# Encoder layer in split fp32r on one core: all late low parts of weight tiles made on VectorE

## The chip, the cores and the metric

The kernel runs on one core of a Trainium2 chip. Its time is device microseconds of one execution. A time is the median of several executions; beside them one execution is taken with the hardware profiler, and that one has a time of its own.

## The reference

One layer of a hybrid encoder is applied to two groups with shared weights: a prompt of 512 tokens and a sample of 1024, width 1024. All values are fp32. Cut to what matters:

```python
h = rms_norm(x, g_pre) * (1 + scale) + shift
p = h @ w_in
a_val, a_glu, a_z, u, v, b_z, g_a, g_b = jnp.split(p, IN_SPLITS, axis=-1)
y_a = conv_branch(a_val, a_glu, a_z, ...)   # GLU, depthwise conv of 31, LayerNorm, silu, gate, projection
y_b = sgu_branch(u, v, b_z, ...)            # u * (w_s v + b) per chunk of 128, gate, projection
m = jax.nn.sigmoid(g_a) * y_a + jax.nn.sigmoid(g_b) * y_b
o = m @ w_out
return x + gate * rms_norm(o, g_post)
```

So there are eight 1024x1024 products for the combined projection, two for the branches' own projections and one for the output, each for 512 + 1024 tokens.

## The kernel before

**Products.** TensorE multiplies fp32r numbers, which hold less than an fp32. Each fp32 operand is therefore split into a high part (a cast to fp32r) and a low part (the operand less its high part, again as fp32r), and each product is made of three matmuls: high by high, high by low, low by high. A step for one block of 128 output channels is 24 matmuls of 128x128 by 128x512. A unit of weights is a tile of 128x1024 that SyncE loads into `raw`; ScalarE casts it into `hi` (L247), and `lo` = `raw` - `hi` is made in one of three ways. The rings of `raw`, `hi` and `lo` hold four tiles each.

**Three ways to the low part.** `unit_act` and `unit_dve` do it. With `by_dma` true, ScalarE writes the rounded negative of `raw` into `lo`, and a transfer issued by GpSimd adds `raw` to it (L254, L240). With `by_dma` equal to "gp", GpSimd subtracts (L250). With `by_dma` false, VectorE subtracts (L263, in `unit_dve`). Which way a unit goes is set by the number of its step: up to `CONV_END` = 72 by the transfer, from there on the even steps by GpSimd and the odd ones by VectorE. The weights of the sample's `pair`s (below) are made in their own way, and the change does not touch them.

**Order of the steps.** The prompt comes first, in 88 steps: its combined projection, and from step 72 the branches' own projection (`cproj`) and the output projection (`w_out`). The sample is cut into two halves of 512 tokens, `sa` and `sb`. `steps_v` makes v of `sa` and of `sb` (16 steps). Then 28 `pair`s make the other products of the sample: each multiplies two channel blocks for both halves with seven half-size products of 12 matmuls (X, Y, X, Z, X, Z, X, on the operands (0,0), (0,1), S2, S1, S3, S4, (1,1)). S1 to S4 are sums of quarters of the activation; the generator `prep2` makes S3, S1, S2 in four rounds, one for each slice of 128 rows: four sums (L938 to L941), a subtraction (L933) and two of L935 for the low parts. The fourth sum is stored, and `prep3` loads it again for S4 (L971). At the end come `post_B` of `sa` and `sb`, `post_A` of `sa`, `steps_o` of `sa`, `post_A` of `sb` and `steps_o` of `sb` (48 steps).

**Background work and the planner.** A planner in Python writes the program, in the order in which the engines then run it. It keeps clocks of its own (`clk["pe"]`, `clk["dve"]`, `clk["act"]`); `dv(cost, ...)` emits an instruction of VectorE and adds its cost. After each step it emits that step's own work on ScalarE and VectorE, and `fill` puts in pieces of background work (generators in the list `bg`) as long as VectorE's planned clock is behind a given time. The prompt's convolution, `prep2`, `prep3`, `late_ln` and other jobs of the sample are such work. If a step needs a job that isn't finished, `meet` (L1424) calls `force`, which runs that job to its end there: the first `pair` needs "S" with its third product (L1063), and the first step of `post_A` needs hA of its half (L1331). `late_ln` makes hA: L1261 multiplies a block by the gate, ScalarE casts it, L1253 makes its low part; eight blocks.

**Names that the prediction uses.** L549 to L561 are the LayerNorm of v at the end of `steps_v` (L545 on ScalarE reads its banks from PSUM). L1028 adds two products of a `pair`; L1077 to L1084 and L1100 make that `pair`'s weights. L404 to L407 are the convolution. L623 to L640 end the output projection of a half. L336 and L335 are small matmuls that spread a mean over the rows, L325 makes their low part. L572 mixes v along the tokens.

Of the kernel before, what the change touches and what calls it, by code (L numbers as in the profile page):

```python
# [17 lines left out]
F32 = mybir.dt.float32  # L18
# [3 lines left out]
ALU = mybir.AluOpType  # L22
# [21 lines left out]
CONV_END = 72  # L44
# [36 lines left out]
def layer_kernel(ctx: ExitStack, tc, x_p, x_s, xt_p, xt_a, xt_b, par, w_blk, w_v, cproj, sproj, w_out, w_ada, w_gate, wsT, bs,  # L81
# [13 lines left out]
    V, S, PE, SP, GP = nc.vector, nc.scalar, nc.tensor, nc.sync, nc.gpsimd  # L95

    def bank():
        return ps.tile([P, T], F32, tag="b", name="b")

    def wk(n=T, dt=F32):  # L100
        return wkp.tile([P, T], dt, tag="wk", name="wk")[:, :n]

    def slot():
        return s16.tile([P, NK, T], F32, tag="s", name="S")
# [10 lines left out]
    def tok(t):  # L115

        return t.rearrange("p (i h) d -> p i (h d)", i=4)
# [10 lines left out]
    def dv(cost, fn):  # L128
        fn()
        clk["dve"] += cost  # L130
# [72 lines left out]
    steps = []  # L203
# [9 lines left out]
    def part_tile(n):  # L213
        return ring.tile([P, D], F32R, tag=n, name=n)

    live = {"raw": 0}
# [17 lines left out]
    def have(u):  # L234
        while u.raw is None:
            unit_load(loadq.pop(0)[1])

    def lo_by_dma(lo, src):

        GP.dma_start(lo.bitcast(F32), src, accum_op=ALU.add)  # L240

    def unit_act(u):
        if u.hi is None:
            have(u)
            u.hi = part_tile("hi")
            u.lo = part_tile("lo")
            S.copy(u.hi, u.raw)  # L247
            clk["act"] += 0.96
            if u.by_dma == "gp":
                GP.tensor_tensor(out=u.lo, in0=u.raw, in1=u.hi.bitcast(F32), op=ALU.subtract)  # L250
                u.raw = True
                live["raw"] -= 1
            elif u.by_dma:
                S.activation(u.lo, u.raw, AF.Copy, scale=-1.0)  # L254
                clk["act"] += 0.96
                lo_by_dma(u.lo, u.raw)
                u.raw = True
                live["raw"] -= 1
# [187 lines left out]
    def mm_cols(dst, u, act):  # L446
        wh3 = u.hi.rearrange("p (k c) -> p k c", k=NK)
        wl3 = u.lo.rearrange("p (k c) -> p k c", k=NK)
        for k in range(NK):
            if k == NK // 2:  # L450
                poll(clk["pe"] - PLAIN / 2)
            hi, lo = act.hi(k), act.lo(k)
            PE.matmul(dst, lhsT=wh3[:, k, :], rhs=hi, start=(k == 0), stop=False)  # L453
            PE.matmul(dst, lhsT=wh3[:, k, :], rhs=lo, start=False, stop=False)  # L454
            PE.matmul(dst, lhsT=wl3[:, k, :], rhs=hi, start=False, stop=(k == NK - 1))  # L455

    def mm_quarter(dst, wh, wl, act, q):
        for i in range(2):
            k = 2 * q + i
            hi, lo = act.hi(k), act.lo(k)  # L460
            PE.matmul(dst, lhsT=wh[:, i, :], rhs=hi, start=(k == 0), stop=False)
            PE.matmul(dst, lhsT=wh[:, i, :], rhs=lo, start=False, stop=False)
            PE.matmul(dst, lhsT=wl[:, i, :], rhs=hi, start=False, stop=(k == NK - 1))
# [28 lines left out]
    def add_step(st, *units):  # L492

        steps.append(st)
        st.units = units
        return st

    def col_step(t, src, act, a1=None, d1=None, d2=None, a2=None, pre=None, box=None, need=None, by_dma=True):
        u = Unit(src, len(steps), by_dma and (len(steps) < CONV_END or (len(steps) % 2 == 0 and "gp")))

        def mm():
            b = bank()
            mm_cols(b, u, act())
            box[0] = b

        st = add_step(Step(mm, a1, d1, a2, d2, pre, need=need), u)

        def quarter(b, wh, wl, q):
            box[0] = b
            mm_quarter(b, wh, wl, act(), q)  # L510
        st.quarter = quarter
        return st
# [15 lines left out]
    def steps_v(t, need=None):  # L528

        for h in range(2):  # L530
            banks = []
            for kc in range(4):
                u = Unit(w_v[h, kc], len(steps), True if len(steps) < CONV_END else len(steps) % 2 == 0 and "gp")

                def mm(u=u, kc=kc, banks=banks):
                    if kc == 0:
                        banks[:] = [bank() for _ in range(4)]
                    mm_rows(banks, u, t.operand(), kc)

                def a1(h=h, banks=banks):  # L540
                    if h == 0:
                        t.v = t.v_home()
                        t.bn = smp.tile([P, 4, 12], F32, tag="bn", name="bn", bufs=1)
                    for i in range(4):
                        S.activation(t.v[:, i, h * T:(h + 1) * T], banks[i], AF.Gelu_apprx_tanh)  # L545

                def d1(h=h):
                    for i in range(4):
                        dv(0.65, lambda: V.bn_stats(out=t.bn[:, i, h * 6:h * 6 + 6], in_=t.v[:, i, h * T:(h + 1) * T]))  # L549

                def d2(h=h):
                    if h == 0:
                        return
                    mv = smp.tile([P, 4, 2], F32, tag="mv", name="mv")
                    for i in range(4):
                        dv(0.15, lambda: V.bn_aggr(out=mv[:, i, :], in_=t.bn[:, i, :].rearrange("p (c s) -> p c s", s=6)))
                    var = smp.tile([P, 4], F32, tag="ss", name="var")
                    dv(0.1, lambda: V.tensor_copy(var, mv[:, :, 1]))
                    r = rstd_small(var, 4, LN_EPS)
                    for i in range(4):  # L560
                        dv(0.65, lambda: V.tensor_scalar(t.v[:, i, :], t.v[:, i, :], mv[:, i, 0:1], r[:, i:i + 1],  # L561
                                                         op0=ALU.subtract, op1=ALU.mult))
                    if t.after_v:
                        t.after_v()
                last = kc == 3
                add_step(Step(mm, a1 if last else None, d1 if last else None, None, d2 if last else None,
                              act=2.2 if last else 0.0, need=need if h == 0 and kc == 0 else None), u)
# [20 lines left out]
    def steps_o(t, final, on_end=None):  # L588

        for h in range(2):  # L590
            banks = []
            for kc in range(4):
                u = Unit(w_out[h, kc], len(steps), True if len(steps) < CONV_END else len(steps) % 2 == 0 and "gp")

                def mm(u=u, h=h, kc=kc, banks=banks):
                    if kc == 0:
                        banks[:] = [bank() for _ in range(4)]
                    if final and h == 1 and kc >= 1:
                        t.wl.append(u)
                        if kc == 3:  # L600
                            for i in range(4):
                                for c in (1, 2, 3):
                                    mm_rows(banks, t.wl[c - 1], t.m, c, (i,))
                        return
                    mm_rows(banks, u, t.m, kc)

                def a1(h=h, kc=kc, banks=banks):
                    if kc == 3:
                        if h == 0:
                            t.o = tok(slot())  # L610
                            t.q = smp.tile([P, 2, 4], F32, tag="q", name="q")
                        junk = wk()
                        for i in range(4):
                            S.activation(junk, banks[i], AF.Square, scale=1.0 / 32, accum_out=t.q[:, h, i:i + 1])

                def d1(h=h, kc=kc, banks=banks):
                    if kc == 3:
                        if h == 1 and final:
                            out_last(t, banks)
                            return  # L620
                        c = slice(h * T, h * T + T)
                        for i in range(4):
                            dv(0.6, lambda: V.tensor_mul(t.o[:, i, c], banks[i], G[t.g][:, c]))  # L623
                        if h == 1:
                            bg.insert(0, out_gen(t))
                st = add_step(Step(mm, a1, d1, act=2.3 if kc == 3 else 0.0), u)
                if h == 0 and kc == 0:
                    def start():
                        out_load(t)
                        t.o_begun = True  # L630
                    st.extra = start
# [856 lines left out]
    raw = {}  # L1488
# [134 lines left out]
    for q in range(4):  # L1623
        for j in range(NH):
            u = q * NH + j
# [215 lines left out]
```

## Time and profile before

| | us |
|---|---|
| median of three executions | 1452.87 (1452.58 to 1463.46) |
| the profiled execution | 1456.93 |
| its span | 1455.2 |
| TensorE busy in it | 1430.6 |
| VectorE busy | 1195.0 |
| ScalarE busy | 703.4 |
| GpSimd busy | 252.2 |

The span runs from the first instruction to the last; the remaining 1.7 us of the execution lie around it. L12 is line 12 of the kernel; `b` is a bank of PSUM, `wk` a tile of 128x512, `A` an operand for TensorE with its high and low part, `c` a tile of convolution or v. In a row of single instructions stand start, duration, engine, line, operation, and in brackets the idle time before it and what ended that. In a row of waits stand the total, the number of waits and the longest. In a row of stretches stand the start and end, the length, the busy time of TensorE, its weight loads, VectorE, ScalarE and GpSimd (the number of instructions in brackets), the granted clock of TensorE, the share of the DMA engines and GB/s.

### The profile page before, as it was taken

The numbers are of one execution on the slowest core, as the hardware profiler recorded it, in microseconds if no ns is written. First come the engines' busy times: TensorE is split into PE (matmuls) and PEld (weight loads), VectorE is DVE, ScalarE is ACT, GpSimd is POOL, SyncE is SP. The second block draws the span as 40 slices with busy tenths as digits, with TensorE's granted clock in tenths as the row PEclk, the third lists the DMA queues.
The fourth block names the chain that finished last, engine by engine and source line by source line (L and its number), as shares of the span: only waits on it lengthen the run. The fifth ranks groups of instructions, "written<-read, shape, count | busy, mean of one in ns | idle before, by whom it ended". The sixth has DMA issues, their size and how long they took to land.

```text
span 1455.2 us, 17663 instructions
## 1 busy us (share of the span) xinstructions
PE 1430.6 (98%) x6332; PEld 1169.5 (80%) x6332; DVE 1195.0 (82%) x1600; ACT 703.4 (48%) x1020; POOL 252.2 (17%) x216
## 2 busy tenths in 40 slices
PE   8999999999999999999999999999999999999997
PEld 4688888888878888888888888788888887888886
DVE  6769999975348876967999997899999969789855
ACT  4533644554475343454455555455556544444432
POOL 0001111111112221111111111111111122222120
PEclk9999999999999999999999999999999999999999
DMA  9277986898995556666667877898887797455451
GB/s 340 84 217 194 233 212 166 200 255 183 255 251 177 215 183 246 231 164 198 168 140 184 211 187 185 245 254 227 229 234 192 192 304 272 161 219 184 153 206 58
DMA packets 113703, 298.60 MB, mean 205 GB/s; under 512 B 12624, under 2 KB 16336, under 8 KB 112848
## 3 DMA queue, kind: packets, MB, share of 16 engines
q1 hardware_dynamic: 88992, 229.85, 46.0%
q0 software_dynamic: 24624, 67.64, 25.6%
q8 instruction: 49, 0.80, 0.2%
q14 instruction: 38, 0.31, 0.1%
HBM read 182.10 MB, written 47.71 MB: 158 GB/s over the span
## 4 chain that ended last, share of the span: by engine, by line
PE 74%; DVE 10%; DMA 9%; issue 3%; ACT 2%; SPq 1%; DVEq 0%; ACTq 0%; POOLq 0%
PE b L455 10%; PE b L453 10%; PE b L454 10%; PE b L487 9%; PE b L489 9%; PE b L488 9%; PE b L476 4%; PE b L477 4%; PE b L478 4%; DMA wk<-d 3%; DMA raw<-in_w_blk_dram 2%; DVE c L407 2%; PE b L572 1%; DMA raw<-in_w_v_dram 1%; DMA c<-d 1%
## 5 line engine op out<-in xcount | busy, mean ns | idle before, releaser
L487 PE MATMUL b<-A,hi 128*128 128x512 f32 x784 | 306.8, 391 | 3.9 <-ACT wk L1024 3.7
L488 PE MATMUL b<-A,hi 128*128 128x512 f32 x784 | 306.0, 390 | 0.0
L489 PE MATMUL b<-A,lo 128*128 128x512 f32 x784 | 306.0, 390 | 0.0
L453 PE MATMUL b<-A,hi 128*128 128x512 f32 x776 | 303.2, 391 | 0.0
L455 PE MATMUL b<-A,lo 128*128 128x512 f32 x776 | 302.1, 389 | 0.1
L454 PE MATMUL b<-A,hi 128*128 128x512 f32 x776 | 302.1, 389 | 0.0
L407 DVE SCALAR_TENSOR_TENSOR c<-c,prm 128x1024 f32<-128x1024 f32 x240 | 297.7, 1281 | 0.6
L247 ACT CAST hi<-raw 128x1024 fp32r<-128x1024 f32 x145 | 152.2, 1050 | 244.8 <-DMA raw<-in_w_v_dram 67.1
L487 PEld LDWEIGHTS b<-A,hi 128*128 128x128 f32 x784 | 147.8, 189 | 35.7 <-ACT wk L1024 5.1
L488 PEld LDWEIGHTS b<-A,hi 128*128 128x128 f32 x784 | 147.9, 189 | 30.9 <-DVE A L971 0.2
L489 PEld LDWEIGHTS b<-A,lo 128*128 128x128 f32 x784 | 147.7, 188 | 30.6
L455 PEld LDWEIGHTS b<-A,lo 128*128 128x128 f32 x776 | 145.7, 188 | 31.0 <-DMA lo<-raw 0.6
L454 PEld LDWEIGHTS b<-A,hi 128*128 128x128 f32 x776 | 145.7, 188 | 30.3 <-issue 0.2
L453 PEld LDWEIGHTS b<-A,hi 128*128 128x128 f32 x776 | 145.7, 188 | 30.2 <-issue 0.2
L407 DVE SCALAR_TENSOR_TENSOR S<-c,prm,S 128x512 f32<-128x512 f32 x240 | 162.5, 752 | 0.4
L250 POOL TENSOR_TENSOR lo<-raw,hi 128x1024 fp32r<-128x1024 f32 x40 | 103.8, 2596 | 329.9 <-ACT hi L247 322.3
L240 POOL DMA_DIRECT2D lo<-T x84 | 72.6, 865 | 456.6 <-ACT lo L1089 366.9
L476 PE MATMUL b<-hi,A 128*128 128x512 f32 x384 | 150.6, 392 | 0.0
L477 PE MATMUL b<-lo,A 128*128 128x512 f32 x384 | 149.8, 390 | 0.0
L478 PE MATMUL b<-hi,A 128*128 128x512 f32 x384 | 149.7, 390 | 0.0
L240 POOL DMA_DIRECT2D lo<-raw x87 | 75.4, 866 | 383.7 <-ACT lo L254 359.4
L1024 ACT COPY wk<-b 128x512 f32<-128x512 f32 x112 | 65.7, 586 | 125.3 <-PE b L489 117.3
(207 smaller groups left out, 1766.0 us busy)
## 6 DMA issues: line engine op xcount, KB each, us to landing
raw<-in_w_blk_dram SPq DMA_DIRECT2D x105, 512.0 KB, 5.3
d<-wk SPq DMA_DIRECT2D x142, 256.0 KB, 3.2
lo<-raw POOLq DMA_DIRECT2D x59, 512.0 KB, 6.1
wk<-d SPq DMA_DIRECT2D x116, 256.0 KB, 5.2
lo<-T POOLq DMA_DIRECT2D x28, 512.0 KB, 4.6
lo<-T POOLq DMA_DIRECT2D x56, 256.0 KB, 4.5
raw<-in_w_v_dram SPq DMA_DIRECT2D x24, 512.0 KB, 5.8
raw<-in_sproj_dram SPq DMA_DIRECT2D x24, 512.0 KB, 5.0
```

Of the source, the lines that this page charges most:

```text
L240: GP.dma_start(lo.bitcast(F32), src, accum_op=ALU.add)
L247: S.copy(u.hi, u.raw)
L407: lambda: V.scalar_tensor_tensor(acc, in0=win, scalar=wt, in1=acc, op0=ALU.mult, op1=ALU.add))
L453: PE.matmul(dst, lhsT=wh3[:, k, :], rhs=hi, start=(k == 0), stop=False)
L454: PE.matmul(dst, lhsT=wh3[:, k, :], rhs=lo, start=False, stop=False)
L455: PE.matmul(dst, lhsT=wl3[:, k, :], rhs=hi, start=False, stop=(k == NK - 1))
L476: PE.matmul(banks[i], lhsT=hi, rhs=wh3[:, kk, :], start=(k == 0), stop=False)
L477: PE.matmul(banks[i], lhsT=hi, rhs=wl3[:, kk, :], start=False, stop=False)
L478: PE.matmul(banks[i], lhsT=lo, rhs=wh3[:, kk, :], start=False, stop=(k == NK - 1))
L487: PE.matmul(dst, lhsT=wh3[:, k, :], rhs=hi, start=st, stop=False, skip_group_check=True)
L488: PE.matmul(dst, lhsT=wh3[:, k, :], rhs=lo, start=False, stop=False, skip_group_check=True)
L489: PE.matmul(dst, lhsT=wl3[:, k, :], rhs=hi, start=False, stop=sp, skip_group_check=True)
```

## The change

The branch in which GpSimd subtracts is taken out of `unit_act`. The units that took it (40, which are half of those from step 72 on: 8 of the prompt's last 16 steps, 8 of the two `steps_v`, 24 of the last 48 steps) are now made by VectorE in `unit_dve`, and the planner adds 1.14 to VectorE's clock for each, where it added nothing to any clock for GpSimd's.

```diff
@@ -246,11 +246,7 @@
             u.lo = part_tile("lo")
             S.copy(u.hi, u.raw)
             clk["act"] += 0.96
-            if u.by_dma == "gp":
-                GP.tensor_tensor(out=u.lo, in0=u.raw, in1=u.hi.bitcast(F32), op=ALU.subtract)
-                u.raw = True
-                live["raw"] -= 1
-            elif u.by_dma:
+            if u.by_dma:
                 S.activation(u.lo, u.raw, AF.Copy, scale=-1.0)
                 clk["act"] += 0.96
                 lo_by_dma(u.lo, u.raw)
@@ -496,7 +492,7 @@
         return st
 
     def col_step(t, src, act, a1=None, d1=None, d2=None, a2=None, pre=None, box=None, need=None, by_dma=True):
-        u = Unit(src, len(steps), by_dma and (len(steps) < CONV_END or (len(steps) % 2 == 0 and "gp")))
+        u = Unit(src, len(steps), by_dma and len(steps) < CONV_END)
 
         def mm():
             b = bank()
@@ -530,7 +526,7 @@
         for h in range(2):
             banks = []
             for kc in range(4):
-                u = Unit(w_v[h, kc], len(steps), True if len(steps) < CONV_END else len(steps) % 2 == 0 and "gp")
+                u = Unit(w_v[h, kc], len(steps), len(steps) < CONV_END)
 
                 def mm(u=u, kc=kc, banks=banks):
                     if kc == 0:
@@ -590,7 +586,7 @@
         for h in range(2):
             banks = []
             for kc in range(4):
-                u = Unit(w_out[h, kc], len(steps), True if len(steps) < CONV_END else len(steps) % 2 == 0 and "gp")
+                u = Unit(w_out[h, kc], len(steps), len(steps) < CONV_END)
 
                 def mm(u=u, h=h, kc=kc, banks=banks):
                     if kc == 0:
```

Since the clocks change, the planner puts other work at other places. Lines behind the first hunk have numbers four lower in the changed kernel. Two places on VectorE follow. The first is the passage from `steps_v` of `sb` to the first `pair`. Before, the last round of `prep2` stood between the two halves of v of `sb`, whose first L549 is the top row here:

```order
L549 BN_STATS bn<-c_4796 128x6 x4
L263 TENSOR_TENSOR lo<-raw,hi 128x1024
L938 TENSOR_TENSOR wk<-wk 128x512
L939 TENSOR_TENSOR wk<-wk 128x512
L940 TENSOR_TENSOR wk<-wk 128x512
L941 TENSOR_TENSOR wk<-wk 128x512
L1077 TENSOR_TENSOR T_4850<-raw 128x512
L1078 TENSOR_TENSOR T_4850<-raw,T_4850 128x512
L1100 TENSOR_TENSOR lo<-raw,hi 128x1024
L933 TENSOR_TENSOR A<-wk,A 128x512
L935 SCALAR_TENSOR_TENSOR A<-wk,s_t,A 128x512
L1083 TENSOR_TENSOR T_4885<-raw 128x512
```

and behind the end of v (L561) came the work of the first `pair` and S4 (L971):

```order
L561 TENSOR_SCALAR c_4796<-c_4796,mv,r 128x1024 x4
L1028 TENSOR_TENSOR wk<-b,wk 128x512
L1077 TENSOR_TENSOR T_5033<-raw 128x512
L1078 TENSOR_TENSOR T_5033<-raw,T_5033 128x512
L1100 TENSOR_TENSOR lo<-raw,hi 128x1024
L1083 TENSOR_TENSOR T_5071<-raw 128x512
L1084 TENSOR_TENSOR T_5071<-raw,T_5033 128x512
L971 TENSOR_TENSOR A<-wk,A 128x512
L1032 TENSOR_TENSOR wk<-wk 128x512
```

After the change, behind the end of v (now L557):

```order
L557 TENSOR_SCALAR c_4768<-c_4768,mv,r 128x1024 x4
L1024 TENSOR_TENSOR wk<-b,wk 128x512
L1073 TENSOR_TENSOR T_5007<-raw 128x512
L1074 TENSOR_TENSOR T_5007<-raw,T_5007 128x512
L1096 TENSOR_TENSOR lo<-raw,hi 128x1024
L934 TENSOR_TENSOR wk<-wk 128x512
L935 TENSOR_TENSOR wk<-wk 128x512
L936 TENSOR_TENSOR wk<-wk 128x512
L937 TENSOR_TENSOR wk<-wk 128x512
L929 TENSOR_TENSOR A<-wk,A 128x512
L931 SCALAR_TENSOR_TENSOR A<-wk,s_t,A 128x512 x2
```

The round of four sums (L934 to L937 now), the subtraction and the two of L931 have moved from ahead of v's end to behind the first weights of the first `pair`.

The second place is the end of `steps_o` of `sa`, ahead of `post_A` of `sb`. Before, the last pieces of hA (L1261, L1253) stood ahead of the second L623:

```order
L263 TENSOR_TENSOR lo<-raw,hi 128x1024
L1261 TENSOR_TENSOR wk<-wk,c_10114 128x512
L1253 TENSOR_TENSOR A<-wk,A 128x512
L1261 TENSOR_TENSOR wk<-wk,c_10114 128x512
L1253 TENSOR_TENSOR A<-wk,A 128x512
L1261 TENSOR_TENSOR wk<-wk,c_10114 128x512
L1253 TENSOR_TENSOR A<-wk,A 128x512 x2
L623 TENSOR_TENSOR S<-b,G_9838 128x512 x4
L640 SCALAR_TENSOR_TENSOR ss<-q 128x4
```

After the change the second L623 is L619, and ahead of it stand only these pieces of hA:

```order
L1257 TENSOR_TENSOR wk<-wk,c_10141 128x512 x2
L259 TENSOR_TENSOR lo<-raw,hi 128x1024
L1249 TENSOR_TENSOR A<-wk,A 128x512
L1257 TENSOR_TENSOR wk<-wk,c_10141 128x512
L1249 TENSOR_TENSOR A<-wk,A 128x512
L619 TENSOR_TENSOR S<-b,G_9837 128x512 x4
L636 SCALAR_TENSOR_TENSOR ss<-q 128x4
```

and behind it, after the ten small operations that end in L165:

```order
L165 SCALAR_TENSOR_TENSOR r<-u,r 128x4
L259 TENSOR_TENSOR lo<-raw,hi 128x1024
L1257 TENSOR_TENSOR wk<-wk,c_10141 128x512
L1249 TENSOR_TENSOR A<-wk,A 128x512
L1257 TENSOR_TENSOR wk<-wk,c_10141 128x512
L1249 TENSOR_TENSOR A<-wk,A 128x512
L1257 TENSOR_TENSOR wk<-wk,c_10141 128x512
L1249 TENSOR_TENSOR A<-wk,A 128x512
L1257 TENSOR_TENSOR wk<-wk,c_10141 128x512
L1249 TENSOR_TENSOR A<-wk,A 128x512
L1257 TENSOR_TENSOR wk<-wk,c_10141 128x512
L1249 TENSOR_TENSOR A<-wk,A 128x512 x2
L643 SCALAR_TENSOR_TENSOR S<-S,r 128x1024 x4
```

Five of the eight L1257 (L1261 before) and six of the eight L1249 (L1253 before) have moved behind it.

## The prediction

> **What bounds the kernel now.** I read the page first (span, busy times), then TensorE's waits, then the table by stretches.
>
> ```profile
> span 1455.2 us, 17663 instructions
> PE 1430.6 (98%) x6332; PEld 1169.5 (80%) x6332; DVE 1195.0 (82%) x1600; ACT 703.4 (48%) x1020; POOL 252.2 (17%) x216
> ```
>
> ```profile
> PE b L487 <- ACT wk L1024: 3.7, 2, 3.3
> ...
> PE b L336 <- DVE wk L325: 2.3, 3, 1.4
> PE b L572 <- DVE c L561: 1.8, 4, 1.1
> ```
>
> ```profile
> 500.00:600.00 100.00, 98.24 (x432) 80.96 (x431) 76.19 (x104) 41.31 (x63) 22.14 (x9) 0.98 0.62 215
> 600.00:700.00 100.00, 100.00 (x499) 84.83 (x498) 73.09 (x114) 46.70 (x72) 15.40 (x16) 1.00 0.72 202
> 900.00:1000.00 100.00, 96.61 (x414) 79.13 (x413) 88.05 (x101) 53.26 (x84) 17.27 (x20) 0.97 0.88 237
> 1160.00:1400.00 240.00, 238.04 (x1047) 196.16 (x1047) 203.18 (x250) 108.66 (x158) 57.44 (x25) 1.00 0.65 225
> ```
>
> TensorE (PE) is busy for 1430.6 of 1455.2 us; the second number of a stretch is its busy time. The program ends when TensorE ends, so a change off TensorE matters only through its gaps. All it could still remove in these four stretches is 1.8 + 0.0 + 3.4 + 2.0 = 7.2 us (100 or 240 less its busy time). No wait for a subtracted low part stands among the large ones: what the change touches is not late now.
>
> **The change part by part.** The execution shown took 1456.93 us (span and 1.7 around it), 4.1 above the median of 1452.87. I work with differences and put them on both.
>
> *Forty subtractions move.*
>
> ```profile
> L250 POOL TENSOR_TENSOR lo<-raw,hi 128x1024 fp32r<-128x1024 f32 x40 | 103.8, 2596 | 329.9 <-ACT hi L247 322.3 <-PE b L478 7.6
> L263 DVE TENSOR_TENSOR lo<-raw,hi 128x1024 fp32r<-128x1024 f32 x46 | 56.2, 1221 | 30.7 <-ACT hi L247 30.7
> ```
>
> GpSimd loses 103.8 us; nothing waits for that. VectorE gains 40 x 1.22 = 48.8 us, and perhaps 40 x 30.7/46 = 27 us of waiting at these rows for the cast of the high part. Against this stands what GpSimd's subtractions cost VectorE:
>
> ```profile
> 579.89 2.88 DVE L938 TENSOR_TENSOR wk<-wk 128x512 f32<-128x512 f32 x1
> 596.05 0.69 DVE L938 TENSOR_TENSOR wk<-wk 128x512 f32<-128x512 f32 x1
> L522 DVE TENSOR_TENSOR A<-wk,A 128x512 fp32r<-128x512 f32 x16 | 15.8, 990 | 10.4 <-ACT A L519 10.4
> L1261 DVE TENSOR_TENSOR wk<-wk,c 128x512 f32<-128x512 f32 x16 | 15.1, 952 | 0.0
> ```
>
> The same instruction takes 0.69 us, or 2.88 with a GpSimd subtraction beside it. The last two rows are groups of the stretch 1160 to 1456, where 24 of the 40 run: with 0.69 us for one, their excess is 16 x (0.30 + 0.26) = 9 us. That is a floor for 24 of them, so 15 for 40; the ceiling is one full delay each, 40 x 2.19 = 88. I take the middle, 52, since other lines are stretched too. VectorE then gets 3 us less busy, but waits up to 27 more: between 39 us freed (88 - 49) and 61 lost (49 + 27 - 15), spread over some 450 us in which it idles about a fifth (76.19, 73.09 of 100, 203.18 of 240). By itself I cost this at nothing: idle VectorE hides it, and where that cover is gone it shows as the two gaps below. The Trainium skill, "SBUF — State Buffer", section "SBUF: two separate sides", says that a VectorE instruction with two SBUF inputs and a GpSimd instruction that reads SBUF exclude each other for a whole instruction; 2.88 against 0.69 agrees. By that rule alone the sum would be a small gain; it is the first rival.
>
> *The planner's order moves, and this has the price.* Each moved subtraction charges 1.14 us to the planner's VectorE clock, which was charged nothing for GpSimd's. So `fill` puts less background work between the steps, and a job not finished is pulled in by `meet` only where its step stands.
>
> *Place A, the first product that needs S2.* `meet` pulls the whole last round of the operand S (four sums, one subtraction, two of L935) in behind the second half of the sample's v, as the rows of the order in the section on the change show. Durations, all from before:
>
> ```profile
> 615.89 0.68 DVE L938 TENSOR_TENSOR wk<-wk 128x512 f32<-128x512 f32 x1
> 618.66 0.68 DVE L1077 TENSOR_TENSOR T<-raw 128x512 f32<-128x512 f32 x1
> 621.13 0.68 DVE L933 TENSOR_TENSOR A<-wk,A 128x512 fp32r<-128x512 f32 x1
> 621.73 0.74 DVE L935 SCALAR_TENSOR_TENSOR A<-wk,s_t,A 128x512 fp32r<-128x512 f32 x1
> 633.23 0.39 PE L487 MATMUL b<-A,hi 128*128 128x512 f32 x1
> 633.43 0.60 ACT L545 ACTIVATE c<-b 128x512 f32<-128x512 f32 x1 [0.76 <-PE b L478]
> 634.06 0.69 DVE L549 BATCH_NORM_STATS2 bn<-c 128x6 f32<-128x512 f32 x1 [0.42 <-ACT c L545]
> 637.52 2.98 DVE L561 TENSOR_SCALAR c<-c,mv,r 128x1024 f32<-128x1024 f32 x4
> 640.41 0.69 DVE L1028 TENSOR_TENSOR wk<-b,wk 128x512 f32<-128x512 f32 x1
> 643.48 0.68 DVE L1083 TENSOR_TENSOR T<-raw 128x512 f32<-128x512 f32 x1
> ```
>
> Let E = 633.23 be where v's last matmul gives way to the pair. Everything from L549 on hangs on E (last bank, L545, L549, the small ones, L561). Where before runs L1083, at E + 10.25, the round now begins: four sums 2.77 (615.89 to 618.66), L933 0.60 (621.13 to 621.73), two of L935 at 0.7 each: S2 is there at E + 15.0. TensorE has 34 matmuls before it needs that last slice: the first two products of 12, and three slices of three and one more. At 0.227 us each (below, 1359.08 to 1361.35 for ten) this is E + 7.7. The gap is 7.3 us. Before, it had S2 at 621.73 and soon after, ahead of E, and TensorE is busy 100.00 of this 100 us.
>
> *What hangs behind A.* S4 is loaded back from what the fourth sum of this round stores:
>
> ```profile
> d<-wk SPq DMA_DIRECT2D x142, 256.0 KB, 3.2
> ...
> wk<-d SPq DMA_DIRECT2D x116, 256.0 KB, 5.2
> ```
>
> From E + 13.0 this is 13.0 + 3.2 + 5.2 = E + 21.4, with a cast and a subtraction (0.6 each) E + 22.6; TensorE wants it after 26 more matmuls, at E + 15.0 + 5.9 = E + 20.9 at the earliest, its last slice 9 matmuls later at E + 22.9, and later with a slow clock: no further gap counted.
>
> *What a gap costs beyond itself.*
>
> ```profile
> 920.81 0.39 PE L489 MATMUL b<-A,lo 128*128 128x512 f32 x1
> 924.46 0.80 PE L487 MATMUL b<-A,hi 128*128 128x512 f32 x1 [3.26 <-ACT wk L1024]
> 925.05 0.63 PE L488 MATMUL b<-A,hi 128*128 128x512 f32 x1
> 929.74 0.53 PE L487 MATMUL b<-A,hi 128*128 128x512 f32 x1
> ```
>
> After a gap of 3.65 us, TensorE took 5.28 us for the 12 matmuls up to 929.74, which take 2.72 otherwise, in the stretch with granted clock 0.97: 2.6 us more. So A costs 7.3 + 2.6 = 9.9; without the slow stretch 7.3. The Trainium skill, "TensorE: Matmul & The Clock Gate", section "What's actually happening", states half rate after an idle window of about 3.4 us, until some 3.4 us of work; by that a gap costs about 1.7 us more (an estimate from that page) instead of 2.6. The sum would be 0.9 lower; the row decides.
>
> *Place B, the first step of post_A for the sample's second half.* Its operand hA is made by L1261 and L1253, eight of each. Before, the last ran at 1356.32. Now eleven of them stand behind the second half of L623, its small operations and one subtraction.
>
> ```profile
> 1354.65 0.69 DVE L1261 TENSOR_TENSOR wk<-wk,c 128x512 f32<-128x512 f32 x1
> 1355.25 0.69 DVE L1253 TENSOR_TENSOR A<-wk,A 128x512 fp32r<-128x512 f32 x1
> 1356.32 2.47 DVE L1253 TENSOR_TENSOR A<-wk,A 128x512 fp32r<-128x512 f32 x1 [0.39 <-ACT A L1262]
> 1359.08 0.39 PE L476 MATMUL b<-hi,A 128*128 128x512 f32 x1
> 1359.76 0.39 PE L453 MATMUL b<-A,hi 128*128 128x512 f32 x1
> 1361.35 0.39 PE L454 MATMUL b<-A,hi 128*128 128x512 f32 x1
> 1360.74 0.69 DVE L623 TENSOR_TENSOR S<-b,G 128x512 f32<-128x512 f32 x1 [0.16 <-ACT wk L614]
> 1363.44 1.23 DVE L263 TENSOR_TENSOR lo<-raw,hi 128x1024 fp32r<-128x1024 f32 x1
> ```
>
> With E2 = 1359.76 as the end of the step before, L263 ends at 1364.67 = E2 + 4.9 (L623 needs the last bank, so this can't be earlier). Then 11 x 0.60 = 6.6 (1354.65 to 1355.25): the eighth slice is ready at E2 + 11.5. TensorE reaches the third slice at E2 + 6 x 0.227 = 1.4, finds it at E2 + 6.1 and then goes at VectorE's pace; three matmuls after the last slice give E2 + 12.2 to 12.8 instead of 24 x 0.227 = 5.45. B costs 7.1 on average of these; 4.7 if only the first gap counts, 7.4 with slow matmuls to the end.
>
> *What is gained.* The waits at L561 (1.8) and at L336 (2.3) stand where VectorE is behind GpSimd's subtractions. At best both go (with the slow matmuls that follow the first, up to 5.4 together), at worst none: I take 2.5. The wait at L1024 (3.3, with its slow matmuls 3.65 + 2.6 = 6.2) hangs on transfers and stays: 0, between -6.2 and +6.2.
>
> Sum: 9.9 + 7.1 - 2.5 = 14.5 us: 1452.87 + 14.5 = 1467.4, and 1471.4 against the execution shown. Ends without the wait at L1024: 7.3 + 4.7 - 5.4 = 6.6 and 9.9 + 7.4 - 0 = 17.3, so 1459.5 to 1470.2.
>
> **The rivals.**
> First, the other side: VectorE is ahead. The same rows of GpSimd (2.88 against 0.69) are what it is held by; if the relief nears 88 us, and the background work that `fill` puts later is done in time all the same, A and B don't open and the gaps at L561 and L336 go: 1452.87 - 5.4 = 1447.5, up to about 1454. For it: VectorE idles a fifth of these stretches. Against: at both places the late work is chained to E and E2, whatever VectorE did earlier; it decides only if the round stands ahead of L549, which the new order doesn't show. 0.10.
> Second, the gaps open but are shorter: part of the chain overlaps, the clock stays up. 7.3 + 4.7 - 2.5 = 9.5, so 1459 to 1463. 0.17.
> Third, one more gap of the same make, where another job is pulled in late (the pairs after A, the sample's convolution). Priced by the row at 924.46, 3.65 + 2.6 = 6.2: 1473.6. For it: VectorE is 88.05 busy of 100 there, and forty charges of 1.14 shift everything behind. 0.15.
> That the change doesn't do what it says: the branch is gone and VectorE has forty more rows; GpSimd still issues its transfers. 0.01.
>
> **How the numbers follow.** The forecast, both gaps at 1463 to 1471, gets 0.57. The range reaches from the shorter gaps to the near half of the third rival, 1458 to 1474: 0.57 + 0.16 + 0.08 = 0.81. One per cent, about what a measurement of this kernel can tell from no change, is 14.5 us: 1438.3 and 1467.4. My sum lies on the upper line, so the forecast splits into halves. Slower: 0.28 + the third rival 0.14 + 0.02 of others = 0.44. Faster by 14.5 us would need more than the gaps that are left: 0.03. Within: 0.53.
>
> **What would show it.** In the changed profile, whose line numbers are four lower from the edit on: no POOL TENSOR_TENSOR, 46 + 40 rows of VectorE's subtraction at about 1.22; no L938 or L1261 at 2 to 3 us (now L934, L1257); a wait of TensorE for VectorE's L931 (L935 before) of some 7 us in the first pair, with matmuls 0.43 apart behind it; another of 4 to 5 at L449 for L1249; and a granted clock below 1 in these two stretches. A wrong prediction would show TensorE's busy time up with no such waits, waits at the subtractions themselves (L259), or S2 ready in time, with the round ahead of L549.

## The result, and the profile after

| | us |
|---|---|
| before, median of six executions taken with it | 1455.04 (1452.58 to 1463.46) |
| after, median of six executions | 1467.9 (1465.37 to 1469.57) |
| ratio | 1.0083, 95% interval 1.0064 to 1.0101 |
| after, the profiled execution | 1467.77 (before: 1456.93) |

The change costs 12.9 us by the medians; the ratio says 0.83%. The page of the changed kernel (span, busy times) and its table of TensorE's waits (total, times, longest):

```profile
span 1466.1 us, 17639 instructions
...
PE 1432.4 (98%) x6332; PEld 1169.7 (80%) x6332; DVE 1178.2 (80%) x1640; ACT 702.0 (48%) x1020; POOL 148.9 (10%) x176
```

```profile
PE b L450 <- DVE A L1249: 5.8, 1, 5.8
PE b L483 <- ACT A L923: 5.5, 1, 5.5
...
PE b L483 <- ACT wk L1020: 1.9, 4, 0.9
...
PE b L484 <- DVE A L931: 1.1, 1, 1.1
```

VectorE has 40 instructions more and is busy 16.8 us less (1195.0 to 1178.2). No wait of TensorE for a weight's subtraction (L259) is in this table. The new waits are the two that the prediction placed: the operand S2 in the first pair (L923 makes its high part, L931 its low part), and hA at `post_A` (L1249). The stretches show where VectorE became freer and TensorE idler all the same:

```profile
500.00:600.00 100.00, 100.00 (x455) 83.27 (x454) 72.33 (x113) 41.58 (x63) 0.00 (x0) 1.00 0.64 221
600.00:700.00 100.00, 93.35 (x455) 78.70 (x454) 69.88 (x110) 45.49 (x70) 11.45 (x13) 0.97 0.66 188
900.00:1000.00 100.00, 98.91 (x435) 81.22 (x435) 91.62 (x105) 54.91 (x87) 18.40 (x21) 1.00 0.89 247
1160.00:1400.00 240.00, 232.75 (x1013) 190.74 (x1012) 187.44 (x264) 107.50 (x157) 2.58 (x3) 0.99 0.64 216
```

From 600 to 700 us VectorE's busy time falls from 73.09 to 69.88 and TensorE's from 100.00 to 93.35; from 1160 to 1400 from 203.18 to 187.44 and from 238.04 to 232.75. If TensorE waited because VectorE had too much to do, VectorE would be busier here than before, not less busy.

Both traces hold 6332 matmuls, so the start of the n-th can be compared. The difference, after less before, changes only in these stretches (times are those of before):

| stretch | gain or loss of the stretch, us | what is there |
|---|---|---|
| 0 to 456 us | +2.6 | a small matmul at 425 us (L331, L335 before) waits 0.45 us longer; behind it the granted clock is 0.50 for 3.4 us |
| 456 to 609 us | -4.4 | the gap of 1.5 us at 591 us is gone |
| 609 to 668 us | +9.2 | place A |
| 668 to 933 us | -6.6 | the gap of 3.65 us at 921 us is gone (and 0.4 us at 913 us) |
| 933 to 1201 us | +2.9 | small gaps, the largest at 965 us (1.29) and 1052 us (0.95) |
| 1201 to 1226 us | -1.1 | the gap of 1.8 us at 1203 us is gone |
| 1226 us to the end | +8.3 | place B |

The sum is 10.8 us, as the two profiled executions differ (1467.77 - 1456.93). Each trace is one execution, and that of before took 1.9 us more than its median, so the terms add up to 10.8 and not to 12.9.

Place A in single instructions, first TensorE, then VectorE:

```profile
631.38 0.39 PE L483 MATMUL b<-A,hi 128*128 128x512 f32 x1
...
638.63 0.39 PE L485 MATMUL b<-A,lo 128*128 128x512 f32 x1
644.56 0.80 PE L483 MATMUL b<-A,hi 128*128 128x512 f32 x1 [5.54 <-ACT A L923]
646.46 0.79 PE L484 MATMUL b<-A,hi 128*128 128x512 f32 x1 [1.10 <-DVE A L931]
```

```profile
635.66 2.98 DVE L557 TENSOR_SCALAR c<-c,mv,r 128x1024 f32<-128x1024 f32 x4
...
641.62 0.68 DVE L934 TENSOR_TENSOR wk<-wk 128x512 f32<-128x512 f32 x1
...
645.00 1.41 DVE L931 SCALAR_TENSOR_TENSOR A<-wk,s_t,A 128x512 fp32r<-128x512 f32 x2
```

E is 631.38 here. The round of S begins at E + 10.24 (forecast 10.25) and S2 is whole at 646.41, E + 15.03 (forecast 15.0). TensorE runs 33 matmuls, stops at 638.63 and is idle 5.93 + 1.90 less two spacings of 0.23, 7.4 us (forecast 7.3). The rest of the 9.2 us is slow matmuls.

Place B, TensorE, then VectorE and ScalarE:

```profile
1362.26 0.39 PE L449 MATMUL b<-A,hi 128*128 128x512 f32 x1
...
1363.62 0.39 PE L449 MATMUL b<-A,hi 128*128 128x512 f32 x1
1369.85 0.80 PE L450 MATMUL b<-A,hi 128*128 128x512 f32 x1 [5.84 <-DVE A L1249]
```

```profile
1362.51 2.85 DVE L619 TENSOR_TENSOR S<-b,G 128x512 f32<-128x512 f32 x4 [1.37 <-ACT wk L610]
...
1367.37 1.22 DVE L259 TENSOR_TENSOR lo<-raw,hi 128x1024 fp32r<-128x1024 f32 x1
...
1369.11 0.68 DVE L1249 TENSOR_TENSOR A<-wk,A 128x512 fp32r<-128x512 f32 x1
...
1373.93 1.46 DVE L1249 TENSOR_TENSOR A<-wk,A 128x512 fp32r<-128x512 f32 x2
```

```profile
1360.57 0.62 ACT L1258 CAST A<-wk 128x512 fp32r<-128x512 f32 x1
1361.10 0.81 ACT L1244 ACTIVATE c<-c,prm 128x512 f32<-128x512 f32 x1
1361.82 0.58 ACT L610 ACTIVATE wk<-b 128x512 f32<-128x512 f32 x1
```

E2 is 1362.26. The third slice is there at E2 + 7.5 and not at E2 + 6.1, the last at E2 + 13.1 and not at 11.5. The difference stands ahead of L619: VectorE waits 1.37 us for L610 (ScalarE's square of a bank), which runs late behind casts and activations of the same moved job (L1258, L1244). Before, the first three of its four instructions (L623) began ahead of E2 = 1359.76:

```profile
1358.71 1.87 DVE L623 TENSOR_TENSOR S<-b,G 128x512 f32<-128x512 f32 x3
```

Of the 8.3 us at this place 6.0 are the gap (6.23 less one spacing of 0.23). Behind it 1.9 are matmuls 0.43 apart, and 0.4 are waits of the weight loads for the last slices.

### The profile page after: what moved, and what is told of

Read it like the earlier page. It is cut to its first block, busy times and chain, and to the rows that moved or that the text cites. A ratio compares the mean times of both kernels' runs of the same rounds, so it can differ in the third digit from the quotient of the medians.

```text
span 1466.1 us, 17639 instructions
## 1 busy us (share of the span) xinstructions
PE 1432.4 (98%) x6332; PEld 1169.7 (80%) x6332; DVE 1178.2 (80%) x1640; ACT 702.0 (48%) x1020; POOL 148.9 (10%) x176
## 4 chain that ended last, share of the span: by engine, by line
PE 57%; DVE 6%; DMA 3%; issue 1%; ACT 1%; SPq 1%; DVEq 0%; ACTq 0%
PE b L483 10%; PE b L484 10%; PE b L485 10%; PE b L473 5%; PE b L474 5%; PE b L472 5%; PE b L450 4%; PE b L451 4%; PE b L449 4%; DMA wk<-d 2%; PE b L568 1%; DVE c L403 1%; DVE wk L1175 1%; DVE lo L259 0%; DMA d<-c 0%
## 5 line engine op out<-in xcount | busy, mean ns | idle before, releaser
L259 DVE TENSOR_TENSOR lo<-raw,hi 128x1024 fp32r<-128x1024 f32 x86 | 104.9, 1221 | 58.3 <-ACT hi L247 58.1
L1020 ACT COPY wk<-b 128x512 f32<-128x512 f32 x112 | 65.4, 584 | 123.9 <-PE b L485 118.0
```

## The experiments

Two theories. "Order": the time goes because the planner, charged more, puts other work later; VectorE's added work itself costs nothing. "Load": VectorE has 49 us more to do and comes late.

**The order of before, the work on VectorE.** The units that GpSimd had are subtracted by VectorE, and the planner charges nothing for it:

```diff
-            dv(1.14, lambda: V.tensor_sub(w, r, h.bitcast(F32)))
+            dv(0.0 if u.by_dma == "gp" else 1.14, lambda: V.tensor_sub(w, r, h.bitcast(F32)))
```

> VectorE makes the forty low parts, as after the change, but the planner is charged nothing for them, so every engine has its instructions in the order of before, with forty subtractions put in on VectorE. Theory 'order' (the time is lost because the planner puts other work later): neither of the two large gaps of TensorE opens; the gaps at the mixing of v (591 us) and at the small matmuls (1203 us) shrink as they did after the change, worth about 5.3 and 1.7 us; the gap at 921 us stays, since it hangs on transfers whose order is the old one. About 7 us under before: 1448, between 1443 and 1453. Rival 'load' (VectorE has 49 us more to do and is late with it): the gaps open all the same, about as after the change, 1463 to 1470. Rival 'no relief': within 2 us of before.

Measured: 1450.91 us, ratio to before 0.9962 (0.9947 to 0.9977). Apart from the forty subtractions, TensorE, VectorE, ScalarE and GpSimd run the same instructions in the same order as in the trace of before. Neither large gap opens. So forty subtractions more on VectorE are not what costs time; with the order kept, the move is a gain of about 5 us, and this version beats both kernels. TensorE's first waits in its table:

```profile
PE b L483 <- ACT wk L1020: 3.9, 3, 3.0
...
PE b L331 <- ACT wk L320: 1.3, 1, 1.3
```

The 3.0 is the gap at 921 us, which stayed, as expected of the old order.

**The order of after, the work on GpSimd.** Here only the planner's clock is told:

```diff
+        if u.by_dma == "gp":
+            dv(1.14, lambda: None)
         if not u.by_dma and u.raw is not True:
```

> GpSimd makes the forty low parts, as before the change, but the planner charges 1.14 to VectorE's clock for each, so every engine has its instructions in the order of after the change, without the forty subtractions on VectorE. Theory 'order': both large gaps open (5.9 + 1.9 us ahead of the third product of the first pair, 6.2 us at the first step of post_A of the second half), and VectorE is held by GpSimd besides: 1466 to 1475, about 1470. Rival 'load': without the added work VectorE is in time, no such gap, 1451 to 1458.

Measured: 1473.8 us, ratio 1.0122 (1.0103 to 1.0141). Apart from the subtractions, the four engines run in the order of the changed kernel's trace. A kernel with not one instruction moved between engines loses 17.9 us by its order alone. Its waits (line numbers are two higher than before's):

```profile
PE b L456 <- DVE A L1255: 7.1, 1, 7.1
PE b L489 <- ACT A L929: 5.5, 1, 5.5
```

The gap at place A is the same to 0.01 us as after the change (5.93 and 1.90 from matmul to matmul). At B it is longer by 1.2 us: there one L1255 of VectorE takes 2.48 us beside a subtraction of GpSimd. The four kernels make a square:

| medians, us | order of before | order of after | order costs |
|---|---|---|---|
| GpSimd subtracts | 1455.88 | 1473.8 | +17.9 |
| VectorE subtracts | 1450.91 | 1467.9 | +17.0 |
| the work on VectorE costs | -5.0 | -5.9 | |

**No subtraction at all**, in the order of before; the matmuls read the high part where the low part would stand:

```diff
             if u.by_dma == "gp":
-                GP.tensor_tensor(out=u.lo, in0=u.raw, in1=u.hi.bitcast(F32), op=ALU.subtract)
+                u.lo = u.hi
                 u.raw = True
```

> Leaves the forty subtractions out altogether: the matmuls with the low part of these forty weight tiles read the high part instead, as many as before; the order on every engine is that of before. What it costs the kernel to have them made at all. Theory 'order': the same as with VectorE in the old order to within 3 us (1445 to 1451), since VectorE's idle time hides forty subtractions; the gaps at 591 and 1203 us shrink, the one at 921 us stays. If VectorE's load counts, it is faster than that one by more than 4 us. If GpSimd's subtractions cost nothing, it is within 2 us of before.

Measured: 1450.19 us, ratio 0.9961 (0.9949 to 0.9974). Against 1450.91 with VectorE in the same order, the work costs nothing that can be measured. Its page gives the price of GpSimd's subtractions to VectorE: 1195.0 us busy before, here

```profile
PE 1425.1 (98%) x6332; PEld 1165.5 (80%) x6332; DVE 1132.7 (78%) x1600; ACT 701.2 (48%) x1020; POOL 148.1 (10%) x176
```

so 62.3 us for 40, 1.56 each.

**Only the first sixteen, only the last 24.** The parts moved are set by the number of the step, 104 being the first pair:

```diff
-len(steps) % 2 == 0 and "gp"
+(len(steps) % 2 == 0 and len(steps) >= 104) and "gp"
```

> Only the sixteen subtractions of the prompt's last steps and of the sample's v move to VectorE (and are charged); the last 24 stay with GpSimd. In the order the round of S stands behind v's end, as after the change, and hA's pieces are back ahead of the end of the output projection. Theory 'order': the gap ahead of the first pair's third product (5.9 + 1.9 us, with the slow clock 10) is there, the one at post_A (6.2) is not; the gap at 591 us is gone (5.3), the one at 921 too (6.6, as in both kernels with the new order), small ones come (about 6): 1455.5 + 10 - 5.3 - 6.6 + 6 = 1459.6, between 1456 and 1463. Rival 'load': sixteen subtractions are 16/40 of 49 us, a loss of 5 with no such gap in that place, or gaps at the subtractions themselves.

Measured: 1460.89 us, ratio 1.0047 (1.0032 to 1.0062). One wait of 5.6 us for S2, none for hA, the gaps at 591 and 921 gone. The other part has `< 104` there:

> Only the 24 late subtractions move to VectorE (and are charged); the sixteen of the prompt's last steps and of the sample's v stay with GpSimd. Theory 'order': up to 1160 us it is the kernel before, gaps at 591 and 921 us included; the one of 6.2 at post_A opens, 8.3 in all, and the small matmuls at 1203 and 1224 us gain about 1.5: 1455.5 + 8.3 - 1.5 = 1462.3, between 1459 and 1465. Rival 'load': 24/40 of any loss, spread, with no gap at that place.

Measured: 1459.71 us, ratio 1.0034 (1.002 to 1.0048). One wait for hA, none for S2, and the gap at 921 us is back. The gap at 591 us, expected to stay, is not: VectorE is 0.23 us late there at most, with the order and GpSimd's instructions of before. So this gap is not a fixed price of GpSimd's subtractions. From the two tables of waits, first sixteen, then last 24:

```profile
PE b L487 <- ACT A L927: 5.6, 1, 5.6
```

```profile
PE b L454 <- DVE A L1253: 5.8, 1, 5.8
```

So the sixteen charges of the prompt's end and of v make gap A, the 24 late ones make gap B.

**Gap B repaired alone.** In the changed kernel a step before the end is told to need hA:

```diff
     steps_o(sa, False)
+    steps[-2].need = ("hA", sb)
```

> The changed kernel, but the step before the last of the first half's output projection is told to need hA of the second half, so the planner runs its pieces ahead of the last L619. Theory 'order': the gap of 6.2 us at post_A goes with the slow matmuls behind it (8.3 in all), the one at the first pair stays: 1467.9 - 8.3 = 1459.6, between 1456 and 1463. Rival 'load': the output projection's end comes late instead, 1465 to 1469.

Measured: 1458.01 us, ratio 1.0018 (1.0004 to 1.0031); 9.9 less than the changed kernel's median, and 8.0 by comparing matmuls of the traces: -8.3 at place B, and +0.3 elsewhere.

**Gap A repaired alone: a miss.**

```diff
     steps_v(sb, need=[(p1, (1, 1)), (p2, (1, 0))])
+    steps[-3].need = "S"
```

> The changed kernel, but the third step from the end of the second half's v is told to need S, so the planner runs the last round of S ahead of v's end; nothing else is told. Theory 'order': the gap ahead of the first pair's third product goes with its slow stretch (10 us), the 6.2 at post_A stays: 1467.9 - 10 = 1458, between 1454 and 1461. Rival 'load': VectorE has no time for it there either, and the gap moves to v's own normalization or the mixing: 1464 to 1469.

Measured: 1470.88 us, ratio 1.0117 (1.0102 to 1.0132): 3 us worse than the changed kernel. It looked like the rival's case. In its trace the gap at place A has given way to one of 9.9 us ahead of the first pair's third product, which adds to a bank that L1020 has to copy first. ScalarE and TensorE there:

```profile
633.34 0.62 ACT L963 CAST A<-wk 128x512 fp32r<-128x512 f32 x1 [2.95 <-DMA wk<-d]
637.32 0.62 ACT L963 CAST A<-wk 128x512 fp32r<-128x512 f32 x1 [3.35 <-DMA wk<-d]
639.29 0.62 ACT L963 CAST A<-wk 128x512 fp32r<-128x512 f32 x1 [1.36 <-DMA wk<-d]
641.34 0.62 ACT L963 CAST A<-wk 128x512 fp32r<-128x512 f32 x1 [1.42 <-DMA wk<-d]
641.86 2.05 ACT L541 ACTIVATE c<-b 128x512 f32<-128x512 f32 x4
643.78 0.61 ACT L1020 COPY wk<-b 128x512 f32<-128x512 f32 x1
```

```profile
634.51 0.39 PE L485 MATMUL b<-A,lo 128*128 128x512 f32 x1
644.44 0.79 PE L483 MATMUL b<-A,hi 128*128 128x512 f32 x1 [9.55 <-ACT wk L1020]
```

S2 was in time: the round had run from 622.72 to 627.5. But S being done, the planner also brought forward `prep3`, and the four casts of S4 (L963), which wait for transfers, now stand ahead of v's activation (L541) and the copy of the pair's first product (L1020). Neither theory as stated: the order again, on another engine. By the matmuls' starts this place costs 3.2 us more than gap A did. The gap at 921 us is also back (3.06 us from matmul to matmul, 6.0 us with its slow matmuls), and smaller places gain 5.3.

**Both repaired,** with the same defect:

> Both of these needs are told. Theory 'order': both gaps go, 1467.9 - 18.4 = 1449.5, between 1446 and 1453, as much as VectorE with the old order (1450.9). Rival 'load': not under 1456.

Measured: 1462.08 us, ratio 1.0058 (1.0043 to 1.0073), with a gap of 10.2 us at 634 us, the one at 921 us back (2.94), and none at `post_A`. It isn't the 1449.5 expected, for the reason just shown. With `prep3` begun one step later:

```diff
-    also(len(steps) - 1, lambda: bg.insert(0, p3))
+    v_end = len(steps)
...
+    also(v_end + 0, lambda: bg.insert(0, p3))
```

> As the kernel with both needs told, but prep3, which reloads S4, is put among the background jobs one step later, with the first pair, so that the casts of S4 on ScalarE stand behind the copies of the first two products and not ahead of v's activation. Theory 'order': the gap of 10.2 us at 634 us came from ScalarE waiting at those casts (L963) for their transfers with v's activation (L541) queued behind; it goes, and no other opens in its place: 1462.1 less the 10.2 and its slow stretch 2.6 gives 1449.3, between 1446 and 1453. Rival 'load': VectorE has no room for the round ahead of v's end, and a gap of several us stays in the first pair: 1456 to 1463.

Measured: 1450.53 us, ratio 0.9971 (0.996 to 0.9981). Both large gaps are gone, and the one at 921 us is too. In its trace, which is that of its slowest execution (1455.85), the largest waits of the `pair`s are one at 964 us and one in the first pair:

```profile
PE b L483 <- ACT wk L1020: 2.3, 1, 2.3
...
PE b L485 <- DMA lo<-T: 1.1, 1, 1.1
```

VectorE with all its charges and forty subtractions is as fast here as with the old order (1450.91). Load is excluded as the cause at both places.

## Why the prediction held

The direction, the size (14.5 forecast, 12.9 measured) and both places came out as worked. By its terms, measured in the traces, which differ by 10.8:

- **Forty subtractions moved cost nothing by themselves: right.** VectorE with them and without them, 1450.91 and 1450.19. What GpSimd's subtractions held up was 62 us of VectorE, within the bounds of 15 and 88 and above the 52 taken.
- **Gap A, 7.3 + 2.6 = 9.9: right in the gap, 7.4; the slow stretch was 1.8,** so 9.2 in all. TensorE's first stop is for the high part from ScalarE (L923), a step that the prediction didn't follow; the second, for L931, sets the end as worked out. The 1.7 that the prediction took from the Trainium skill's rule on the clock ("TensorE: Matmul & The Clock Gate", section "What's actually happening") came nearer here than the row of the gap at 921 us. That is this trace only: behind the same gap the stretch cost 2.2 us with GpSimd in the new order and with B repaired, and 2.9 with the first sixteen. S4 made no further gap, as worked out.
- **Gap B, 7.1: mis-sized, 8.3.** The chain on VectorE was right, but the prediction took L623 from the trace of before, where only its last instruction had to wait for TensorE's end. The moved job has a part on ScalarE, which held L610 back, so all four ran behind E2. That put the first gap at 6.0 and not 4.7. A job that is moved has to be followed on each of its engines.
- **Gaps that vanish, -2.5: undersized.** At 591 and 1203 us it was -4.4 - 1.1 = -5.5, near the bound of 5.4 that the prediction gave. Not all of the first is relief from GpSimd: with the last 24 moved alone the gap was gone too.
- **The gap at 921 us, taken as 0 within 6.2: it went, -6.6.** The four traces with the order of before in that stretch (before, the two others in the old order, the last 24 alone) show it at 3.4 to 3.65 us, the four with the new order (after, GpSimd in the new order, the first sixteen, B repaired) don't. In the two versions with the round early but `prep3` not late it is back, at 3.06 and 2.94. That the order decides it was named only as possible. What it costs is not fixed by the order: with nothing subtracted and with the last 24 moved it cost under 0.2 us beyond itself, in the trace of before 2.7.
- **Small losses of +2.6 and +2.9 weren't in the sum.** The second lies with waits for the copies of the products (L1020). The one at 965 us stands in all four traces with the new order and in none of the old, the one at 1052 us in two of the four. For the first, at 425 us, the gap varied between 1.2 and 1.8 us from kernel to kernel, in the old order too (1.7 with VectorE subtracting); why it varies stays open.

The gains missed (-3.0 and -6.6) and the losses missed (+1.2, +2.6, +2.9) cancelled to -2.9, and place A as a whole was 0.7 less, which takes 14.5 to the 10.8 of the traces. Single terms were off by up to 6.6, so the closeness of the sum is in part luck. The first rival's mechanism, relief from GpSimd, is real: 5 us in the old order, 5.9 in the new. It didn't decide since both gaps are chained to TensorE's own end, as the prediction had it.

## What to carry to other kernels

When a planner writes the order, a number in its cost table is a change to the program: here 1.14 us charged forty times cost 17 us through order, and the work that it stood for cost nothing. To judge such a change, put the two apart (charge without moving, move without charging) before blaming the engine. When a late job is pulled forward, look at every engine that it runs on and at what it wakes: the first repair of gap A only handed the wait to ScalarE.

## What the runs showed of the hardware

Behind a gap TensorE can run slow for a while: its matmuls are 0.43 us apart, not 0.227, and the granted clock is 0.50. In all the traces the clock changes in steps of 3.41 us. How much this costs did not grow with the gap. Behind gap A it was 1.8 to 2.9 us in four traces, behind gap B 1.5 to 2.9 in four, behind the 9.9 us of the first repair 2.6. The gap at 921 us shows both outcomes:

```profile
919.76:923.17 3.41, 1.44 (x7) 0.86 (x5) 3.41 (x5) 0.00 (x0) 0.00 (x0) 1.00 0.48 165
923.17:930.00 6.83, 5.54 (x13) 4.38 (x14) 6.79 (x10) 3.58 (x5) 0.86 (x1) 0.50 0.53 114
```

```profile
915.15:918.56 3.41, 1.72 (x8) 1.10 (x6) 3.41 (x5) 0.00 (x0) 0.00 (x0) 1.00 0.48 175
918.56:921.97 3.41, 1.95 (x8) 1.61 (x9) 3.38 (x5) 2.89 (x4) 0.28 (x1) 1.00 0.30 95
921.97:925.39 3.42, 3.42 (x16) 2.80 (x15) 3.42 (x5) 0.70 (x2) 0.58 (x1) 1.00 0.70 134
```

Above is the trace of before, below the last 24 alone; the stretches are steps of the clock. Before, the gap of 3.65 us leaves TensorE busy for 1.44 us of one step, and the clock is halved in the two steps behind it. With the last 24 moved, the gap of 3.54 us lies across two steps, both busy for about half, and the clock stays whole. So where a gap falls in the steps counts, not only its length.

A much shorter gap can bring the slow clock too. In the trace of before, 1.12 us of idle time and three short ones among the small matmuls of the mixing (L572) were enough:

```profile
592.98 0.46 PE L572 MATMUL b<-wsT_t,c 128*128 128x128 f32 x2 [1.12 <-DVE c L561]
...
596.83 0.77 PE L476 MATMUL b<-hi,A 128*128 128x512 f32 x1
597.40 0.63 PE L477 MATMUL b<-lo,A 128*128 128x512 f32 x1
597.83 0.63 PE L478 MATMUL b<-hi,A 128*128 128x512 f32 x1
```

```profile
592.09:595.50 3.41, 1.88 (x10) 1.33 (x10) 3.41 (x5) 1.73 (x2) 0.79 (x1) 1.00 0.56 227
595.50:598.92 3.42, 3.42 (x14) 3.03 (x13) 3.39 (x3) 0.98 (x2) 3.42 (x1) 0.50 0.00 0
```

The matmuls behind them are 0.43 us apart. Of the 4.4 us that this place was worth, 2.7 are the pauses from matmul to matmul and 1.7 the slow clock. By the Trainium skill ("TensorE: Matmul & The Clock Gate", section "What's actually happening") the rate halves after an idle window of about 3.4 us; these rows differ, since TensorE was busy for 1.88 of the 3.41 us before the clock fell, and they decide here. No exact share is shown: in the traces steps that were busy for 0.50 to 0.57 were followed by either clock.
